# Split weight tiles start 64 or 192 bytes behind a 256-byte edge where they are stationary

## The chip, the cores and the metric

The kernel runs on one core of one Trainium2 chip. The metric is the device time of one execution in microseconds; three runs of the kernel before gave 2508.59, 2505.05 and 2508.44 us, so the median is 2508.44 us.

## The reference, cut to what matters

The reference is two transformer blocks in float32 on 256 tokens of width 2048. The first block is a sliding-window attention and a gated feed-forward layer of width 5632. The second block has an mLSTM layer and then a banded attention. Nearly all of the work is products of the 256 x 2048 activations with large weight matrices. Those whose product the change touches are the query and key columns of `w_in` in the mLSTM layer, the key columns of `kv_w`, and both halves of the attention's `w_in`:

```
def mlstm_mixer(h, w_in, conv_w, conv_b, gate_b, g_head, w_out):
    proj = h @ w_in
    qk = silu(causal_conv(proj[..., :A_V0], conv_w, conv_b))     # query and key columns
    v, o, z = proj[..., A_V0:A_O0], proj[..., A_O0:A_Z0], proj[..., A_Z0:A_G0]
    ...
    return y @ w_out

def second_block(x, c, ...):
    ...
        kv = hkv @ kv_w
        k_sh, v_sh = kv[..., :B_WIDTH], kv[..., B_WIDTH:]
        y = band_attention_mixer(h, k_sh, v_sh, b_w_in[j], b_rel[j], b_w_out[j])
    x = x + gate * rmsnorm(y, g_post[l])

def band_attention_mixer(h, k, v, w_in, rel_table, w_out):
    qz = h @ w_in
    q, z = qz[..., :B_WIDTH], qz[..., B_WIDTH:]
    o = chunk_band_attention(q, k, v, rel_table)
    return (o * silu(z)) @ w_out
```

## The kernel before, in words

**The products.** A weight matrix is read in chunks of 512 columns (`CW`), and a chunk in slots of 256 rows, each one DMA of 512 KB on SyncE's queue into a tile `w` (128 partitions, two row blocks of 512 columns, 4096 bytes in a partition; three buffers). `stream_split` makes two float32r tiles of each: ScalarE copies `w` to `wh`, VectorE writes the remainder `w - wh` to `wl` (four buffers each). The activations lie split in the same way, as `xh` and `xl` for what comes from the residual and `ah` and `al` for what comes from within a layer; each of these holds 16 blocks of 128 x 256 values, 1024 bytes in a partition per block. TensorE then makes three products per pair of blocks: high by high, high by low and low by high.

**The two modes.** `products` (L267) has two orders. In mode "tok" a block of activations (128 tokens) is stationary, that is loaded into TensorE, and 512 weight columns are streamed past it. In mode "wst" it is the other way round: 128 columns of `wh` or `wl` are stationary and the 256 tokens of `xh` or `xl` are streamed, so that the result comes out transposed. Every matmul has a load of its own. Twenty chunks are of mode "wst", each of 16 row blocks x 4 column groups x 3 products = 192 matmuls: eight of query and key columns (`qk_done`, one for each mLSTM head), four of keys (`k_done`) and eight of queries and gates (`qb_done`, `zb_done`). All other chunks are "tok".

**The names in the profile.** A row names the tile written, then the streamed tile, then the loaded one: `mm<-xh,wh` is "wst" (`xh` streams, `wh` is loaded), `mm<-wh,xh` is "tok". `bg` is the PSUM tile of everything else: transposes, attention, and the column sums of `mv_reduce` (L390), in which `acch` and `accl` stream past the constant `onesr`. Since every engine call passes through the wrapper `Eng`, nearly all rows have the line L66.

**Order and addresses.** The order of all instructions is worked out while the program is built: `do_group` takes the slots one after another, and a small model of the engines' clocks (`Clock`, `Eng`) decides between which matmuls the background tasks stand. It knows the shapes and not the addresses. In a partition the tiles of the pool `keep` come first, then those of `strm` (`w`, `wh`, `wl`, `mvt`), then `rest`, `small` and a pool per layer. In the built program all of `xh`, `xl`, `ah`, `al`, `wh` and `wl` start on a multiple of 256 bytes, and so does each block or column group of them that a matmul of a chunk reads. `onesr` starts 128 bytes behind such an edge, `acch` and `accl` 192 bytes.

**The end.** After the last chunks `fin_half` (L1235) squares each PSUM result on ScalarE to get its sum of squares (`sumsq`, L458); the squares themselves go to a scratch tile `sq` of the layer's pool that nobody reads.

Of the kernel before, what the change touches and what calls it, by code (L numbers as in the profile page):

```python
# [10 lines left out]
F32 = mybir.dt.float32  # L11
F32R = mybir.dt.float32r
# [6 lines left out]
P = 128  # L19
# [2 lines left out]
KD = D // P  # L22
SL = 2
CW = 512
NEG = -1.0e30
EPS = 1e-6
DFF = 5632
# [53 lines left out]
def kernel(ctx: ExitStack, tc: tile.TileContext, i: dict, out: bass.AP):  # L81
# [6 lines left out]
    strm = ctx.enter_context(tc.tile_pool(name="strm", bufs=1))  # L88
    rest = ctx.enter_context(tc.tile_pool(name="rest", bufs=1))
    small = ctx.enter_context(tc.tile_pool(name="small", bufs=4))  # L90
    psp = ctx.enter_context(tc.tile_pool(name="psp", bufs=8, space=PSUM))

    live = [0, 0]
    mmres = [4]
    ver = {"x": [0] * KD, "a": [0] * KD}
# [21 lines left out]
    xh = keep.tile([P, KD, T], F32R, name="xh")  # L117
# [15 lines left out]
    order = []  # L133
# [4 lines left out]
    def stream_load(upto):  # L138
        while cnt["load"] < min(upto, len(order)):
            ch, s = order[cnt["load"]]  # L140
            w = strm.tile([P, SL, CW], F32, tag="w", bufs=3, name="w")
            ch.load(s, w)
# [3 lines left out]
    def stream_split(upto):  # L146
        while cnt["split"] < min(upto, len(order)):
            j = cnt["split"]
            w = loaded.pop(j)
            clk.cur = 0.0  # L150
            wh = strm.tile([P, SL, CW], F32R, tag="wh", bufs=4, name="wh")
            S.copy(wh, w)
            wl = strm.tile([P, SL, CW], F32R, tag="wl", bufs=4, name="wl")
            V.tensor_sub(wl, w, wh.bitcast(F32))
            split[j] = (wh, wl, clk.cur)
            cnt["split"] += 1
# [54 lines left out]
    def wload(w, r0, c0):  # L211
        def f(s, t):
            a = w[r0 + s * SL * P:r0 + (s + 1) * SL * P, c0:c0 + CW]
            nc.sync.dma_start(out=t, in_=a.rearrange("(k p) n -> p k n", p=P))
# [11 lines left out]
    def do_group(idxs):  # L226
        staged = len(idxs) > 1
        ch, s0 = order[idxs[0]]
        for k in range(s0 * SL, (s0 + len(idxs)) * SL):
            while ver[ch.need[0]][k] < ch.need[1][k]:  # L230
                stall()
        stream_load(idxs[0] + 1 + PF)
        stream_split(idxs[0] + 1 + SP)
        if s0 == 0:
            shp = [P, CW] if ch.mode == "tok" else [P, 2, T]
            while live[0] + live[1] > 6:
# [3 lines left out]
        for ts in ((0,), (1,)) if staged else ((0, 1),):  # L240
            for j, idx in enumerate(idxs):
                s = order[idx][1]
                if j and ts[0]:
                    stream_load(idx + 1 + PF)
                    stream_split(idx + SP)
                wh, wl, t_w = split.pop(idx) if ts[-1] else split[idx]
                for k in range(SL):
                    kt = s * SL + k
                    clk.cur = max(t_w, rdy[ch.need[0]][kt])
                    products(ch, kt, k, wh, wl, ts)  # L250
                    ch.k = kt + ts[-1]
                    if not staged:
                        mv_step()
                    if kt < ch.nk - 1:
                        pump()
            if s == ch.ns - 1:
                clk.cur = clk.eng["pe"]
                if ch.part is not None:
                    for t in ts:
                        ch.part(ch.ps, t)  # L260
                if ts[-1]:
                    if not (ch.done and ch.done(ch.ps)):
                        mm_free()
                    ch.ps = None
                pump()
# [52 lines left out]
    def mv_jobs():  # L318
        for lab, w, c0, b, kind, dst in (
                [("A", i["ada0"], j * CW, i["ada_b"][0:1, j * CW:(j + 1) * CW], "col", (0, j // 4, j % 4))  # L320
                 for j in range(8)]
# [134 lines left out]
        return b.rearrange("p a b -> p (a b)")  # L456

    def sumsq(junk_pool, src, dst, scale=1.0):  # L458
        j = junk_pool.tile([P, CW], F32, tag="sq", bufs=1, name="sq")
        S.activation(j, src, ACTF.Square, scale=scale, accum_out=dst)  # L460

    def xt_pair(m):
# [83 lines left out]
    ssx = rest.tile([P, 2, 4], F32, name="ssx")  # L546
# [208 lines left out]
    def resid(n, ps, pool, after):  # L755
        for t in range(2):
            c = x[:, t, n * CW:(n + 1) * CW]
            V.tensor_add(c, ps[t], c)
            sumsq(pool, c, ssx[:, t, n:n + 1])
        add_bg(after(n))  # L760
# [36 lines left out]
    pools = {}  # L797
# [50 lines left out]
    def down_part(ps, t):  # L848
        c = x[:, t, 3 * CW:]
        V.tensor_add(c, ps[t], c)  # L850
        sumsq(pools["q2"], c, ssx[:, t, 3:4])
        if t:
            add_bg(xt_raw(3, raw))
# [146 lines left out]
    def num_task(h, v):  # L1000
# [22 lines left out]
        for t in range(2):  # L1023
            sumsq(q3, nm[t], ss[:, t:t + 1], scale=rd[:, t:t + 1])
# [143 lines left out]
    def band_head(g, j):  # L1168
# [5 lines left out]
        nc.sync.dma_start(out=bi, in_=bass.AP(tensor=rel.tensor, offset=h * 383, ap=[[1, P], [1, T]]))  # L1174
        G.memset(bi[0:64, 0:64], NEG)
        yield 1
# [57 lines left out]

    def fin_half(ps, t, n):  # L1235
        c = pools["yy"][:, t, n * CW:(n + 1) * CW]
        sumsq(pools["q4"], ps[t], ssx[:, t, n:n + 1])
        V.tensor_mul(c, ps[t], gt[1][:, n * CW:(n + 1) * CW])

    def fin_done(n):  # L1240
        def f(ps):
            for t in range(2):
                fin_half(ps, t, n)
        return f

    def fin_part(ps, t):
        fin_half(ps, t, 3)
        x_rstd((t,))
        for n in range(4):
            c = x[:, t, n * CW:(n + 1) * CW]  # L1250
            y = pools["yy"][:, t, n * CW:(n + 1) * CW]
            if n == 3:
                S.activation(y, y, ACTF.Copy, scale=rst[:, t:t + 1])
                G.tensor_add(c, c, y)
            else:
                V.scalar_tensor_tensor(c, y, rst[:, t:t + 1], c, op0=ALU.mult, op1=ALU.add)
        for n in range(4):
            nc.sync.dma_start(out=out[t * P:(t + 1) * P, n * CW:(n + 1) * CW], in_=x[:, t, n * CW:(n + 1) * CW])
# [39 lines left out]
    S.activation(warm, ones[:, 0:1], ACTF.Exp)  # L1298
    stream_load(1)
    stream_split(1)  # L1300
    load_x(0)
    nc.sync.dma_start(out=cols, in_=i["cols"])
# [35 lines left out]
def _lay(inputs):  # L1338
# [10 lines left out]
    r = np.arange(P)  # L1349
    lo = np.where(r[None, :] <= r[:, None], f(0), f(NEG)).astype(f)  # L1350
    up = np.where(r[None, :] > r[:, None], f(0), f(NEG)).astype(f)
    ge = np.where(r[None, :] >= r[:, None], f(0), f(NEG)).astype(f)
    inv = np.power(10000.0, -np.arange(0, 64, 2) / 64.0).astype(f)
# [33 lines left out]
```

## Time and profile before

| | |
|---|---|
| median of three runs | 2508.44 us |
| the profiled execution, its own time | 2509.79 us |
| its span, first to last instruction | 2508.0 us |
| mean granted clock of TensorE | 0.989 |
| TensorE busy: matmuls, loads | 2438.4 us (97%), 2076.4 us (83%) |
| VectorE, ScalarE, GpSimd busy | 1752.8 us (70%), 1210.1 us (48%), 173.4 us (7%) |
| share of the matmuls in the chain that ended last | 77% |

"PE" is TensorE's matmuls, "PEld" its loads, which overlap them. A matmul's row lasts from its start until its result is out, and the next one starts long before that; the pace of a run of matmuls is therefore read from their starts and not from their durations. [...]

### The profile page before, as it was taken

Reading aid. Unit: us, or ns where it says so; the run is one execution under the profiler, and the core shown is the slowest. Engines: PE = TensorE matmul, PEld = TensorE weight load, DVE = VectorE, ACT = ScalarE, POOL = GpSimd, SP = SyncE. Lnnn points to the kernel's source line nnn. Section 1 sums busy time; section 2 is a strip of 40 time slices with the busy share of each in tenths; the row PEclk is TensorE's granted clock in tenths of the full one; section 3 lists DMA queues with packets and bytes.
Section 4 is the critical chain, followed back from the end, with each engine's and each line's share of the span. In section 5 each row is a group of like instructions: output and inputs, shape, how many; then the busy total and the mean of one; then the engine's idle time right before and its main releaser. Section 6 shows DMA issues by size and latency. Waiting matters only on the chain.

```text
span 2508.0 us, 34570 instructions
## 1 busy us (share of the span) xinstructions
PE 2438.4 (97%) x12782; PEld 2076.4 (83%) x12782; DVE 1752.8 (70%) x2577; ACT 1210.1 (48%) x1654; POOL 173.4 (7%) x174
## 2 busy tenths in 40 slices
PE   8989999999999999899999999999999899999998
PEld 6867888887888888778888788888888789899986
DVE  6885777777777777768778777755454664577765
ACT  5665544334443444554445444445444544555553
POOL 0232000000000000201101100101101120000000
PEclk9989999999999999999999999999999999999999
DMA  6524788888888887568878788856556456678854
GB/s 211 157 96 143 238 285 284 286 275 279 287 283 291 285 286 267 159 213 269 264 250 273 267 286 277 261 170 192 182 169 196 151 151 186 193 254 263 259 188 153
DMA packets 319226, 575.63 MB, mean 230 GB/s; under 512 B 21680, under 2 KB 56752, under 8 KB 319056
## 3 DMA queue, kind: packets, MB, share of 16 engines
q1 hardware_dynamic: 319056, 573.42, 70.8%
q8 instruction: 100, 1.64, 0.3%
q14 instruction: 70, 0.57, 0.1%
HBM read 571.25 MB, written 2.10 MB: 229 GB/s over the span
## 4 chain that ended last, share of the span: by engine, by line
PE 77%; DVE 7%; DMA 6%; issue 4%; ACT 4%; POOL 2%; SPq 0%; ACTq 0%; DVEq 0%; POOLq 0%
PE mm L66 72%; PE bg L66 5%; DVE wl L66 3%; ACT wh L66 2%; DMA w<-in_a_w_in_dram 2%; DVE mvacc L66 2%; DMA w<-in_w_gate_dram 1%; DMA w<-in_w_down_dram 1%; POOL big L66 1%; DMA w<-in_w_qkv_dram 1%; ACT big L66 1%; POOL y L66 0%; DMA w<-in_a_w_out_dram 0%; POOL so L66 0%; ACT sq L66 0%
## 5 line engine op out<-in xcount | busy, mean ns | idle before, releaser
L66 DVE TENSOR_TENSOR wl<-w,wh 128x1024 fp32r<-128x1024 f32 x816 | 1009.3, 1244 | 620.9 <-ACT wh L66 605.4
L66 ACT CAST wh<-w 128x1024 fp32r<-128x1024 f32 x816 | 854.9, 1051 | 957.1 <-PE mm L66 598.8
L66 PE MATMUL mm<-wh,xh 128*128 128x512 f32 x1760 | 691.4, 393 | 0.0
L66 PE MATMUL mm<-wh,xl 128*128 128x512 f32 x1760 | 686.8, 390 | 3.8 <-DVE xl L66 3.8
L66 PE MATMUL mm<-wl,xh 128*128 128x512 f32 x1760 | 686.8, 390 | 3.0 <-DVE wl L66 3.0
L66 DVE SCALAR_TENSOR_TENSOR mvacc<-mvt,sc,mvacc 128x512 f32<-128x512 f32 x512 | 392.2, 766 | 10.1 <-issue 0.5
L66 PEld LDWEIGHTS mm<-wh,xl 128*128 128x128 f32 x1760 | 331.1, 188 | 74.3 <-DVE xl L66 4.7
L66 PEld LDWEIGHTS mm<-wl,xh 128*128 128x128 f32 x1760 | 331.2, 188 | 72.2 <-DVE wl L66 5.1
L66 PEld LDWEIGHTS mm<-wh,xh 128*128 128x128 f32 x1760 | 331.2, 188 | 70.5 <-issue 2.6
L66 PE MATMUL mm<-xh,wh 128*128 128x256 f32 x1280 | 370.0, 289 | 7.9 <-DVE xh L66 7.9
L66 PE MATMUL mm<-xl,wh 128*128 128x256 f32 x1280 | 367.5, 287 | 1.0 <-DVE xl L66 0.9
L66 PE MATMUL mm<-xh,wl 128*128 128x256 f32 x1280 | 365.6, 286 | 0.0
L66 PE MATMUL mm<-wh,al 128*128 128x512 f32 x864 | 337.8, 391 | 3.5 <-DVE al L66 3.5
L66 PE MATMUL mm<-wh,ah 128*128 128x512 f32 x864 | 340.3, 394 | 0.0
L66 PE MATMUL mm<-wl,ah 128*128 128x512 f32 x864 | 337.5, 391 | 0.0
L66 PEld LDWEIGHTS mm<-xh,wh 128*128 128x128 f32 x1280 | 249.2, 195 | 11.6 <-DVE xh L66 5.5
L66 PEld LDWEIGHTS mm<-xl,wh 128*128 128x128 f32 x1280 | 249.1, 195 | 4.4 <-DVE xl L66 3.5
L66 PEld LDWEIGHTS mm<-xh,wl 128*128 128x128 f32 x1280 | 249.1, 195 | 0.0
L66 PEld LDWEIGHTS mm<-wh,al 128*128 128x128 f32 x864 | 163.0, 189 | 38.1 <-DVE al L66 3.9
L66 PEld LDWEIGHTS mm<-wh,ah 128*128 128x128 f32 x864 | 162.9, 189 | 36.7 <-issue 3.3
L66 PEld LDWEIGHTS mm<-wl,ah 128*128 128x128 f32 x864 | 163.0, 189 | 33.2 <-DVE wl L66 0.3
L66 POOL TENSOR_TENSOR so<-so,sz 128x512 f32<-128x512 f32 x16 | 29.6, 1851 | 711.8 <-DVE mvacc L66 361.8
(191 smaller groups left out, 1303.2 us busy)
## 6 DMA issues: line engine op xcount, KB each, us to landing
mvt<-in_ada_dram SPq DMA_DIRECT2D x192, 512.0 KB
w<-in_a_w_in_dram SPq DMA_DIRECT2D x192, 512.0 KB
w<-in_w_gate_dram SPq DMA_DIRECT2D x88, 512.0 KB
w<-in_w_up_dram SPq DMA_DIRECT2D x88, 512.0 KB
w<-in_w_down_dram SPq DMA_DIRECT2D x88, 512.0 KB
mvt<-in_kv_ada_dram SPq DMA_DIRECT2D x64, 512.0 KB
w<-in_a_w_in_dram SPq DMA_DIRECT2D x128, 256.0 KB
w<-in_a_w_out_dram SPq DMA_DIRECT2D x64, 512.0 KB
```

Of the source, the lines that this page charges most:

```text
L66: return fn(*a, **k)
```

## The change

The buffers of `wh` and `wl` become 256 bytes longer in each partition (`ROOM`, 64 values of four bytes). For a slot of a "wst" chunk the tile that is written and read begins 16 values (64 bytes) into its buffer if the slot's number is even, and 48 values (192 bytes) if it is odd; for a "tok" slot it begins at the buffer's start as before. The eight longer buffers take 2048 bytes more, so every tile behind them moves by 2048 bytes. To make room for that in the last layer, the squares of `fin_half` go into the first two blocks of `xh` instead of a scratch tile. In all five engines' orders the instructions, their shapes and their waits are the same before and after; eight squares name `xh` in place of `sq`. The `wh` and `wl` buffers lie 4352 bytes apart in place of 4096, all still on multiples of 256.

```
+ROOM = 64
+SHIFT = 16
...
+    def offset_tile(tag, off):
+        t = strm.tile([P, SL * CW + ROOM], F32R, tag=tag, bufs=4, name=tag)
+        return t[:, off:off + SL * CW].rearrange("p (k n) -> p k n", n=CW)
...
             j = cnt["split"]
             w = loaded.pop(j)
+            off = SHIFT * (1 + 2 * (j % 2)) if order[j][0].mode == "wst" else 0
             clk.cur = 0.0
-            wh = strm.tile([P, SL, CW], F32R, tag="wh", bufs=4, name="wh")
+            wh = offset_tile("wh", off)
             S.copy(wh, w)
-            wl = strm.tile([P, SL, CW], F32R, tag="wl", bufs=4, name="wl")
+            wl = offset_tile("wl", off)
             V.tensor_sub(wl, w, wh.bitcast(F32))
...
     def sumsq(junk_pool, src, dst, scale=1.0):
-        j = junk_pool.tile([P, CW], F32, tag="sq", bufs=1, name="sq")
+        if junk_pool is None:
+            j = xh[:, 0:2].rearrange("p k t -> p (k t)")
+        else:
+            j = junk_pool.tile([P, CW], F32, tag="sq", bufs=1, name="sq")
         S.activation(j, src, ACTF.Square, scale=scale, accum_out=dst)
...
     def fin_half(ps, t, n):
         c = pools["yy"][:, t, n * CW:(n + 1) * CW]
-        sumsq(pools["q4"], ps[t], ssx[:, t, n:n + 1])
+        sumsq(None, ps[t], ssx[:, t, n:n + 1])
```

## Rows read from the trace of the kernel before

**Rows 1.** The page: span, busy times, GB/s by slice, the chain that ended last.
```profile
span 2508.0 us, 34570 instructions
PE 2438.4 (97%) x12782; PEld 2076.4 (83%) x12782; DVE 1752.8 (70%) x2577; ACT 1210.1 (48%) x1654; POOL 173.4 (7%) x174
...
GB/s 211 157 96 143 238 285 284 286 275 279 287 283 291 285 286 267 159 213 269 264 250 273 267 286 277 261 170 192 182 169 196 151 151 186 193 254 263 259 188 153
...
PE 77%; DVE 7%; DMA 6%; issue 4%; ACT 4%; POOL 2%; SPq 0%; ACTq 0%; DVEq 0%; POOLq 0%
```

**Rows 2.** TensorE's waits, by what ended them: us in total, times, longest.
```profile
PE bg L66 <- POOL y L66: 8.6, 5, 2.2
PE mm L66 <- DVE xh L66: 7.9, 13, 1.9
```

**Rows 3.** Stretches: length, busy us (instructions) by engine, clock, DMA share, GB/s.
```profile
1136.80:1145.40 8.60, 8.60 (x74) 8.60 (x72) 7.04 (x5) 6.45 (x7) 5.04 (x3) 1.00 0.85 278
...
1521.00:1546.00 25.00, 25.00 (x205) 24.71 (x204) 18.49 (x23) 11.44 (x15) 0.53 (x1) 1.00 0.90 289
2040.00:2110.00 70.00, 70.00 (x582) 69.82 (x581) 29.41 (x24) 29.10 (x32) 0.00 (x0) 1.00 0.63 189
2220.00:2408.00 188.00, 187.25 (x1547) 185.62 (x1546) 142.33 (x272) 102.74 (x171) 3.58 (x18) 1.00 0.77 250
```

**Rows 4.** Loads with `xh`, "wst", 2040 to 2105: ns min/median/max, first and last start.
```profile
L66 PEld LDWEIGHTS mm<-xh,wl x181: 192/192/192, 2040.0 to 2104.8; 128*128 128x128 f32 x181
L66 PEld LDWEIGHTS mm<-xh,wh x181: 192/192/192, 2040.2 to 2105.0; 128*128 128x128 f32 x181
```

**Rows 5.** The same in a "tok" stretch, 2110 to 2190.
```profile
L66 PEld LDWEIGHTS mm<-wh,xh x118: 187/188/188, 2110.2 to 2189.8; 128*128 128x128 f32 x118
```

**Rows 6.** The loads of `onesr` for `acch` and for `accl`, whole span, same columns.
```profile
L66 PEld LDWEIGHTS bg<-acch,onesr x16: 186/192/192, 1487.0 to 2400.9; 128*128 128x128 f32 x16
L66 PEld LDWEIGHTS bg<-accl,onesr x16: 186/188/286, 1487.2 to 2401.0; 128*128 128x128 f32 x16
```

**Rows 7.** Loads grouped, 1534.99 to 1536.2: xcount, busy us, mean ns, idle before.
```profile
L66 PEld LDWEIGHTS mm<-xh,wh 128*128 128x128 f32 x4 | 0.8, 188 | 0.0
L66 PEld LDWEIGHTS mm<-xl,wh 128*128 128x128 f32 x3 | 0.6, 188 | 0.0
L66 PEld LDWEIGHTS mm<-xh,wl 128*128 128x128 f32 x3 | 0.6, 187 | 0.0
```

**Rows 8.** Matmuls in time in that stretch: start us, us.
```profile
1534.95 0.28 PE L66 MATMUL bg<-acch,onesr 128*128 128x256 f32 x1
...
1536.38 0.28 PE L66 MATMUL mm<-xl,wh 128*128 128x256 f32 x1
```

**Rows 9.** Loads grouped, 1536.5 to 1545.
```profile
L66 PEld LDWEIGHTS mm<-xh,wl 128*128 128x128 f32 x24 | 4.6, 192 | 0.0
```

**Rows 10.** Matmuls in time, a "tok" stretch behind transposes.
```profile
256.54 0.39 PE L66 MATMUL mm<-wl,ah 128*128 128x512 f32 x1
...
258.85 0.39 PE L66 MATMUL mm<-wh,al 128*128 128x512 f32 x1
```

**Rows 11.** Loads grouped, 2220 to 2408, the chunks of queries and gates.
```profile
L66 PEld LDWEIGHTS mm<-xl,wh 128*128 128x128 f32 x445 | 85.2, 191 | 0.2
```

**Rows 12.** Splits by tile, ns min/median/max: at an edge, then 192 bytes behind one.
```profile
L66 ACT CAST ah<-yb x16: 397/406/407, 2250.3 to 2423.9; 128x256 fp32r<-128x256 f32 x16
L66 DVE TENSOR_TENSOR al<-yb,ah x16: 424/426/427, 2250.8 to 2424.4; 128x256 fp32r<-128x256 f32 x16
...
L66 ACT CAST acch<-mvacc x16: 400/406/408, 1484.4 to 2398.2; 128x256 fp32r<-128x256 f32 x16
L66 DVE TENSOR_TENSOR accl<-mvacc,acch x16: 409/416/427, 1485.6 to 2398.7; 128x256 fp32r<-128x256 f32 x16
```

**Rows 13.** ScalarE's squares of the last chunks, and its casts of `wh`, same columns.
```profile
L66 ACT ACTIVATE sq<-mm x8: 597/598/599, 2447.8 to 2497.8; 128x512 f32<-128x512 f32 x8
...
L66 ACT CAST wh<-w x816: 1027/1053/1078, 4.7 to 2486.6; 128x1024 fp32r<-128x1024 f32 x164
```

**Rows 14.** The transposes of `y` in one query-and-key chunk: start us, us, wait before.
```profile
1145.40 0.27 PE L66 MATMUL bg<-kc,y 128*128 128x128 f32 x1
1147.79 0.98 PE L66 MATMUL bg<-kc,y 128*128 128x128 f32 x7 [2.12 <-POOL y L66]
```

## The prediction

> **What bounds the kernel now.** I read the page first, then the waits, then stretches of time by mode. The reader is to see that TensorE is hardly ever without work: its matmuls are busy for 97% of the span and make up 77% of the chain that ended last [rows 1], and its longest sums of waits are 8.6 and 7.9 us [rows 2]. In the four "wst" chunks of keys it works without a pause at clock 1.00, with 582 matmuls in 70 us [rows 3]. So the time is mostly the number of matmuls times the pace at which they start, and the change can act on the pace only.
>
> The pace of a "wst" stretch comes from the first and last starts: between the loads at 2040.2 and 2105.0 us lie 180 intervals of three matmuls, and 64.8 us / 540 is 120.0 ns [rows 4]. In "tok" 79.6 us / 351 is 226.8 ns [rows 5]. [...] The loads differ: in "wst" each one lasts 192 ns, minimum as maximum, in "tok" 187 to 188 [rows 4, 5]. In "wst" the streaming needs less than the pace, and the next matmul follows its load at a steady distance, 192 - 120 = 72 ns. There I take the load to be what sets the pace: a load of 188 ns would give 116.
>
> **The change part by part.** The term that matters is where the loaded columns lie relative to the streamed ones. Before, both start at an edge in every chunk; after, the loaded ones start 64 or 192 bytes behind it in "wst". The trace never shows that pair, but it shows three near it, where `mv_reduce` streams `acch` and `accl` (192 bytes behind an edge) past `onesr` (128):
> - `onesr` is loaded while `xh` or `wh` streams, distance 128: median 192 ns, as at distance 0 [rows 6].
> - `onesr` is loaded once more while `acch` streams, distance 64: median 188 ns [rows 6].
> - `wh` is loaded while `accl` streams, distance 192: it is the first of four with mean 188 [rows 7].
>
> So distances 0 and 128 go with 192 ns and distances 64 and 192 with 188. The change puts every "wst" load at one of the latter two. A weakness of this reading is that the loads behind such a pair stay at 187 to 188 ns although they are back at distance 0, ten of them [rows 7], and only then return to exactly 192 [rows 9]. What I see may thus be a rhythm that was disturbed and not a distance that is good. The bounds of the new pace: 116 ns by the load (188 - 72), and 119 by the starts of the disturbed stretch (12 intervals in 1.43 us [rows 8]). I take 117, nearer to the load, since the starts include the return to the old rhythm; that is 3 ns less for a matmul.
>
> How many matmuls gain: of the 20 "wst" chunks the first of query and key columns and the first of keys run while VectorE still writes `xh`, with 13 waits on it [rows 2], and what they gain there is waited away. The other 18 have 18 x 192 = 3456 matmuls, and 3456 x 3.0 ns = 10.4 us. Two things are subtracted:
> - In five heads TensorE waits for GpSimd's `y` in the middle of the query-and-key chunk (8.6 us in all [rows 2]; one such place in [rows 14]). In that chunk 74 matmuls stand before the first transpose [rows 3]. Reaching the wait sooner gives nothing: 5 x 74 x 3 ns = 1.1 us.
> - In the eight chunks of queries and gates the mean load is already 85.2 / 445 = 191.5 ns [rows 11], half a nanosecond below 192: 8 x 192 x 0.5 = 0.8 us.
>
> That leaves 8.5 us. Feeding the faster matmuls: in the query-and-key chunks the DMA engines move 289 GB/s at 0.90 busy [rows 3]; at 117 ns they would have to move 296. If 293, the highest of the page's slices [rows 1], were a ceiling, seven chunks would stop at 118.4 ns and 7 x 192 x 1.4 ns = 1.9 us would be lost. I take nothing, since three buffers stand ahead and the "tok" chunks behind need less, and keep 1.9 us for the range.
>
> The smaller parts. The splits write to 64 or 192 behind an edge: a cast of 256 columns takes 406 ns at an edge and 406 at 192 behind it, the subtraction 426 and 416 [rows 12]; zero, and ScalarE and VectorE have slack anyway (103 and 142 us busy in 188 [rows 3]). The eight squares write float32r in place of float32: 598 ns for 512 columns from PSUM now, and a cast that writes float32r takes 1053 for 1024 [rows 13], so the new type costs between nothing and -0.1 us each, of which only the last two lie on the path at the end; zero. They wait for nothing new, as `xh` was last streamed by 2408 us and the first square starts at 2447.8 [rows 13]. The shift of all later tiles by 2048 bytes leaves every distance modulo 256 as it was. The streamed `wh` of "tok" now starts at odd multiples of 256 in two buffers of four; a distance of 128 made no difference to a load, so I take zero for 256.
>
> **The sum.** 2509.79 (the profiled execution, 1.35 above the median) - 8.5 = 2501.3, and against the median 2508.44 - 8.5 = 2499.9; I forecast 2500.
>
> [...]
>
> **The rivals.**
> - The rhythm stays. If 120 ns belongs to the start of a matmul and not to the distance, the "wst" stretches settle at 120 again whatever the offset, and the time is 2508. [...] Against it: distance 64 and 192 show 188 in the very load that has it. That the offset does not do what it says is this case too.
> - Slower. The new offset puts the loads into a worse rhythm and keeps them there. The trace knows such a one: behind transposes a "tok" stretch starts its matmuls at 10 intervals in 2.31 us, 231 ns, 4 above its steady 226.8 [rows 10]. Kept through "wst" that is 3456 x 4 = +13.8 us, 2522. It decides from 1.5 ns per matmul (5 us / 3456). Against it: no disturbed "wst" load in [rows 7] is above 192.
> - A still lower rhythm. The shortest loads are 186 ns [rows 6], so 114: 6 ns x 11 chunks x 192 = 12.7 us outside the query-and-key chunks, and 2.2 us in those if 118.4 is their floor; less the 1.9 us subtracted above, some 13 us, 2495.
>
> **How the numbers follow.** I give the forecast 55%, the rhythm that stays 29%, the slower one 10%, the still lower one 6%. About 0.2%, 5 us, is what a measurement of this kernel can tell from no change. The forecast's own range goes from 116 ns (-12 us, 2496) to 119 with the DMA ceiling (-2.5, 2505.5); roughly one in fifteen of it falls short of 5 us. So faster 0.57, same 0.33, slower 0.10. The range of 8 in 10 runs from 2492, which takes in the lower rhythm and some scatter, to 2511, which takes in the whole of no change with the spread of three runs (3.5 us) and the beginning of the slower case.
>
> **What would show it.** In the profile after, the loads of the key chunks have a median of 187 to 188 ns in place of 192, the 582 matmuls of such a stretch take some 68 us and not 70, and the "tok" stretches keep 226.8 ns. The gain lies in the 18 chunks, 0.5 to 0.6 us each. Loads of 192 at the new offset would prove the first rival, loads above 192 the slower one. The prediction is wrong too if "wst" gains and the waits on `y`, on VectorE or on the weights' DMAs grow by as much, or if "tok" changes its pace.

## The result and the profile after

The changed kernel took 2492.54 us (median of four runs, 2489.58 to 2496.67), the kernel before on the same chip 2506.78 us (four runs, 2505.05 to 2508.59). The ratio is 0.9949 with a 95% interval of 0.9931 to 0.9966, that is a gain of 8.5 to 17.3 us, 12.8 in the middle; the medians differ by 14.2. The forecast was faster, 2500 us, in a range of 2492 to 2511. Sign and range held, the range only just (the median lies 0.5 us above its lower end), and the gain is larger than the 8.5 us forecast. The profiled execution after took 2491.55 us, 18.2 us less than the profiled one before (which lay 3 us above the median it is compared with here).

The page of the kernel after: span, busy times, and the engines' shares of the chain that ended last. Two lines more stand at the top of this kernel, so its rows have L68 where those before have L66.

```profile
span 2489.8 us, 34570 instructions
PE 2418.9 (97%) x12782; PEld 2057.6 (83%) x12782; DVE 1754.3 (70%) x2577; ACT 1209.0 (49%) x1654; POOL 173.6 (7%) x174
...
PE 81%; DVE 6%; DMA 4%; issue 4%; ACT 3%; POOL 2%; SPq 0%; DVEq 0%; ACTq 0%; POOLq 0%
```

Against [rows 1] the instructions are the same in number, TensorE is busy for 19.5 us less, VectorE, ScalarE and GpSimd for the same time as before. TensorE's matmuls still have by far the largest share of the chain, and their busy time got shorter by about what the span got shorter. The next fence has three stretches of the kernel after, with the columns of [rows 3]: a query-and-key chunk, the last three chunks of keys (the first one has waits), and the chunks of queries and gates.

```profile
1516.00:1541.00 25.00, 25.00 (x209) 24.55 (x208) 19.13 (x26) 12.63 (x17) 0.53 (x1) 1.00 0.90 288
2031.00:2095.00 64.00, 64.00 (x568) 64.00 (x567) 29.28 (x24) 27.25 (x29) 0.00 (x0) 1.00 0.66 201
2210.00:2390.00 180.00, 177.90 (x1513) 175.57 (x1512) 140.75 (x272) 100.89 (x171) 3.56 (x18) 1.00 0.79 255
```

In the key chunks 568 matmuls now start in 64 us, where 582 took 70: at the new pace 582 would take 65.6 us, 4.4 less. The clock is 1.00 in each stretch, as it was. Now the loads in the key chunks, in the form of [rows 4], with those of the "tok" stretch behind, in the form of [rows 5].

```profile
L68 PEld LDWEIGHTS mm<-xh,wl x174: 187/188/188, 2031.0 to 2089.8; 128*128 128x128 f32 x174
L68 PEld LDWEIGHTS mm<-xh,wh x174: 187/188/188, 2031.1 to 2089.9; 128*128 128x128 f32 x174
...
L68 PEld LDWEIGHTS mm<-wh,xh x111: 187/188/188, 2100.0 to 2174.8; 128*128 128x128 f32 x111
```

In "wst" 58.8 us / (173 x 3) is 113.3 ns, 6.7 below the 120.0 of before, with loads of 188 ns in place of 192. In "tok" 74.8 us / (110 x 3) is 226.7 ns: unchanged. But 113.3 is not the pace of every "wst" chunk. Two short stretches of an early query-and-key chunk, loads and then matmuls, run otherwise:

```profile
L68 PEld LDWEIGHTS mm<-xh,wl x6: 187/188/188, 1133.0 to 1134.8; 128*128 128x128 f32 x6
...
L68 PE MATMUL mm<-xh,wh x12: 280/281/281, 1131.8 to 1135.7; 128*128 128x256 f32 x12
```

3.9 us / (11 x 3) is 118 ns, with the same loads of 188 ns. What differs is the row of the matmul itself, 281 ns here. In the key chunks of the kernel after, and in those of the kernel before, it has these lengths:

```profile
L68 PE MATMUL mm<-xh,wh x174: 276/276/277, 2030.8 to 2089.7; 128*128 128x256 f32 x174
```

```profile
L66 PE MATMUL mm<-xh,wh x181: 283/283/283, 2039.9 to 2104.7; 128*128 128x256 f32 x181
```

So there are two steady rhythms at the new offsets, 113.3 ns (rows of 276) and 117.8 ns (rows of 281 here), and one at the old offset, 120.0 ns (283). Over all intervals of 110 to 126 ns that begin with a "wst" matmul the mean went from 119.82 ns (3683 of them) to 115.10 (3689): 4.72 ns x 3689 = 17.4 us. "tok" has 227.08 before and 227.07 after.

TensorE's waits of the kernel after, as in [rows 2]: the one on GpSimd's `y` grew by 2.1 us, the one on `xh` by 0.9 (0.8 of it in the first key chunk).

```profile
PE bg L68 <- POOL y L68: 10.7, 5, 2.8
PE mm L68 <- DVE xh L68: 8.8, 10, 2.2
```

The 18.2 us between the two profiles are not all of the change. The first "wst" matmul started at 1023.4 us before and at 1019.1 after, so 4.3 us were ahead of everything that the offset touches. Most of them are a wait on `sg` in the profile before, 3.2 us at 592 us, which does not appear after:

```profile
PE bg L66 <- DVE sg L66: 3.2, 2, 2.9
```

From the first "wst" matmul on, the kernel after was 13.9 us shorter: 17.4 us of pace, less the 3.0 us by which the two waits grew, are 14.4, and the medians differ by 14.2.

### The profile page after: what moved, and what is told of

Its sections match the earlier page's. It is cut to its first block, busy times and chain, and to the rows that moved or that the text cites. A ratio compares the mean times of both kernels' runs of the same rounds, so it can differ in the third digit from the quotient of the medians.

```text
span 2489.8 us, 34570 instructions
## 1 busy us (share of the span) xinstructions
PE 2418.9 (97%) x12782; PEld 2057.6 (83%) x12782; DVE 1754.3 (70%) x2577; ACT 1209.0 (49%) x1654; POOL 173.6 (7%) x174
## 4 chain that ended last, share of the span: by engine, by line
PE 81%; DVE 6%; DMA 4%; issue 4%; ACT 3%; POOL 2%; SPq 0%; DVEq 0%; ACTq 0%; POOLq 0%
PE mm L68 76%; PE bg L68 5%; DVE wl L68 2%; DMA w<-in_a_w_in_dram 2%; ACT wh L68 2%; DVE mvacc L68 1%; POOL big L68 1%; DMA w<-in_w_qkv_dram 1%; POOL so L68 0%; POOL y L68 0%; DMA w<-in_a_w_out_dram 0%; ACT sq L68 0%; ACT big L68 0%; DMA mvacc<-in_ada_b_dram 0%; DVE xl L68 0%
## 5 line engine op out<-in xcount | busy, mean ns | idle before, releaser
L68 DVE TENSOR_TENSOR wl<-w,wh 128x1024 fp32r<-128x1024 f32 x816 | 1010.0, 1245 | 603.6 <-ACT wh L68 590.0
L68 ACT CAST wh<-w 128x1024 fp32r<-128x1024 f32 x816 | 854.9, 1052 | 941.6 <-PE mm L68 633.3
L68 PE MATMUL mm<-wh,xl 128*128 128x512 f32 x1760 | 687.3, 390 | 4.7 <-DVE xl L68 4.7
L68 PE MATMUL mm<-wh,xh 128*128 128x512 f32 x1760 | 691.6, 393 | 0.0
L68 PE MATMUL mm<-wl,xh 128*128 128x512 f32 x1760 | 687.0, 390 | 2.5 <-DVE wl L68 2.5
L68 DVE SCALAR_TENSOR_TENSOR mvacc<-mvt,sc,mvacc 128x512 f32<-128x512 f32 x512 | 392.9, 767 | 10.1 <-DMA mvacc<-in_ada_b_dram 0.9
L68 PEld LDWEIGHTS mm<-wh,xl 128*128 128x128 f32 x1760 | 331.1, 188 | 75.2 <-DVE xl L68 5.9
L68 PEld LDWEIGHTS mm<-wl,xh 128*128 128x128 f32 x1760 | 331.3, 188 | 72.6 <-DVE wl L68 4.9
L68 PEld LDWEIGHTS mm<-wh,xh 128*128 128x128 f32 x1760 | 331.4, 188 | 70.3 <-issue 2.9
L68 PE MATMUL mm<-xh,wh 128*128 128x256 f32 x1280 | 363.6, 284 | 8.8 <-DVE xh L68 8.8
L68 PE MATMUL mm<-xl,wh 128*128 128x256 f32 x1280 | 360.7, 282 | 0.9 <-DVE xl L68 0.7
L68 PE MATMUL mm<-xh,wl 128*128 128x256 f32 x1280 | 359.2, 281 | 0.0
L68 PE MATMUL mm<-wh,al 128*128 128x512 f32 x864 | 337.6, 391 | 4.9 <-DVE al L68 4.9
L68 PE MATMUL mm<-wh,ah 128*128 128x512 f32 x864 | 339.8, 393 | 0.0
L68 PE MATMUL mm<-wl,ah 128*128 128x512 f32 x864 | 337.3, 390 | 0.0
L68 PEld LDWEIGHTS mm<-xh,wh 128*128 128x128 f32 x1280 | 244.8, 191 | 11.9 <-DVE xh L68 6.2
L68 PEld LDWEIGHTS mm<-xl,wh 128*128 128x128 f32 x1280 | 244.8, 191 | 3.8 <-DVE xl L68 3.3
L68 PEld LDWEIGHTS mm<-xh,wl 128*128 128x128 f32 x1280 | 244.5, 191 | 0.0
L68 PEld LDWEIGHTS mm<-wh,al 128*128 128x128 f32 x864 | 162.8, 188 | 39.6 <-DVE al L68 5.3
L68 PEld LDWEIGHTS mm<-wh,ah 128*128 128x128 f32 x864 | 162.8, 188 | 36.6 <-issue 3.3
L68 PEld LDWEIGHTS mm<-wl,ah 128*128 128x128 f32 x864 | 162.7, 188 | 33.2 <-DVE wl L68 0.3
L68 POOL TENSOR_TENSOR so<-so,sz 128x512 f32<-128x512 f32 x16 | 30.6, 1911 | 707.0 <-DVE mvacc L68 360.3
```

Of the source, the lines that this page charges most:

```text
L68: return fn(*a, **k)
```

## The experiments

**Theory and rivals at this point.** Theory: the pace is set by where the loaded columns lie relative to the streamed ones, modulo 128 (0 and 128 alike, 64 and 192 alike). Rivals: what counts is the absolute address of the loaded columns; or any distance but 0 helps; or the alternation from slot to slot is what helps; or the gain is one of the by-products (the longer buffers, the moved tiles, the squares in `xh`).

**Offsets by themselves.** A kernel of matmuls alone: runs of 144 with 256 streamed columns ("wst") and of 96 with 512 ("tok"), all operands in SBUF, each run disturbed beforehand by four or five float32 matmuls. Its core:

```
+    for off in OFFS:                      # 0, 16, 32, ..., 128, 192 bytes
+        for r in range(2):
+            disturb(4 + r)
+            wst(6, [off], 0)              # loaded at off, streamed at 0
+    for offs, mov in (([64, 192], 0), ([0, 128], 0), ([0], 64), ([64], 64)):
...
+    for off in OFFS:
+        for r in range(2):
+            disturb(4 + r)
+            tok(8, off)
```

> Nothing of the blocks is computed here: the kernel holds only runs of matmuls of the two modes, with the loaded columns at an offset of 0, 16, 32, 48, 64, 80, 96, 112, 128 and 192 bytes behind a 256-byte edge, each run behind a few fp32 matmuls; also the streamed columns at 64 with the loaded ones at 0 and at 64, and offsets in turn (64/192 and 0/128). Distance theory (only the distance of the loaded from the streamed columns counts, modulo 128): 120 ns at 0 and 128, 113 to 118 at 64 and 192, the same 113 to 118 with the streamed ones at 64 and the loaded ones at 0, and 120 again with both at 64. Disturbance theory (a change of offset keeps the rhythm from settling): 120 at every constant offset after some ten matmuls, below 118 only with offsets in turn, and there for 0/128 too. For runs of 512 streamed columns both say 226.7 at 0 and 128; the distance theory leaves open whether 64 gives 220 or stays at 226.7.

The pace in the second half of each run (ns, two runs each), from the starts:

| loaded columns at (streamed at 0) | 256 streamed | 512 streamed |
|---|---|---|
| 0 | 120.0, 120.0 | 226.7, 226.7 |
| 16 | 118.3, 118.4 | 233.3, 226.7 |
| 32 | 118.4, 118.4 | 233.3, 233.3 |
| 48 | 123.2, 117.8 | 233.4, 233.3 |
| 64 | 113.3, 117.8 | 233.3, 233.3 |
| 80; 96; 112, twice the same within 0.1 | 118.8; 117.3; 120.0 | 232.0; 234.3; 233.3 |
| 128 | 118.6, 118.6 | 232.4, 232.2 |
| 192 | 117.8, 117.8 | 228.8, 228.8 |
| 64 and 192 in turn, by slot | 113.3, 113.3 | |
| 0 and 128 in turn, by slot | 118.9, 118.9 | |
| 0, streamed at 64 | 117.8, 113.3 | |
| 64, streamed at 64 | 120.0, 120.0 | |

Matmuls of this kernel, one tile of each run; `w064h` is loaded at offset 64, `m064h` streamed at 64. In this order: 0; 64, first and second run; 128; streamed at 64; both at 64.

```profile
L86 PE MATMUL mm<-m000h,w000h x42: 283/283/283, 49.9 to 64.7; 128*128 128x256 f32 x42
...
L86 PE MATMUL mm<-m000h,w064h x45: 276/276/276, 194.9 to 209.9; 128*128 128x256 f32 x45
...
L86 PE MATMUL mm<-m000h,w064h x44: 281/281/281, 212.8 to 228.0; 128*128 128x256 f32 x44
...
L86 PE MATMUL mm<-m000h,w128h x43: 279/281/285, 338.9 to 353.8; 128*128 128x256 f32 x43
...
L86 PE MATMUL mm<-m064h,w000h x44: 276/276/276, 500.1 to 514.7; 128*128 128x256 f32 x44
...
L86 PE MATMUL mm<-m064h,w064h x42: 283/283/283, 518.0 to 532.8; 128*128 128x256 f32 x42
```

The kernel's three rhythms are all here, with VectorE, ScalarE and GpSimd at 0.00 us and the DMA engines at 0.01 of their time at most in these stretches, and with the same lengths of rows: 283, 276, 281. Both at 64 is as both at 0 (120.0 ns), and either of the two may be moved (113.3 and 117.8): the distance counts and not the address. Modulo 128 was wrong: at distance 128 the intervals walk between 115 and 122 ns with a mean of 118.6. Distance 64 twice gave two different paces, each steady to the end of its run. The two runs differ in the number of float32 matmuls ahead, so I read the pace as a matter of how a run was entered. And with 512 columns no offset is better than none: 64 gave 233.3 ns, neither of the two values (220 and 226.7) that the theory had left open.

**One offset for all slots, and none.** Three kernels that differ from the kernel after in one line:

```
-            off = SHIFT * (1 + 2 * (j % 2)) if order[j][0].mode == "wst" else 0
+            off = SHIFT if order[j][0].mode == "wst" else 0          # 64
+            off = 2 * SHIFT if order[j][0].mode == "wst" else 0      # 128
+            off = 0 if order[j][0].mode == "wst" else 0              # 0
```

> The changed kernel with the offset 64 for every wst slot instead of 64 and 192 in turn. Distance theory: about as the changed kernel, 2487 to 2497, wst at 113 to 118 ns. Disturbance theory: wst settles at 120, about 2507.

> The changed kernel with the offset 128 for every wst slot. Distance theory: distance 128 is as 0, wst stays at 120.0 ns and the time at 2505 to 2509. If any offset from the edge of the buffer did it: 2487 to 2497.

> The changed kernel with no offset: the longer buffers, the shift of all later tiles by 2048 bytes and the squares written to xh alone. Distance theory: 120.0 ns and 2505 to 2509. If the gain came from these by-products: 2487 to 2497.

One run each, with the kernel before at 2505.78 us on the same chip: 2492.88 at 64, 2504.08 at 128, 2505.28 at 0. The mean "wst" intervals were 116.15, 119.02 and 119.82 ns. With 0 the time and the pace are those of before, so the longer buffers, the moved tiles and the squares cost and bring nothing that shows. Since its buffers lie 4352 bytes apart, loads at even and at odd multiples of 256 take turns in it, and its key chunks still run at 120 ns: it is the distance modulo 256 that counts. The key chunks at 64, matmuls and loads:

```profile
L68 PE MATMUL mm<-xh,wh x188: 281/281/281, 2028.7 to 2094.8; 128*128 128x256 f32 x188
...
L68 PEld LDWEIGHTS mm<-xh,wl x188: 187/188/188, 2028.8 to 2094.9; 128*128 128x128 f32 x188
```

66.1 us / (187 x 3) = 117.8 ns: entered in the slower rhythm, these chunks kept it to their end, where the kernel after has 113.3. Other chunks of the same kernel ran at 113.3. The key chunks at 128:

```profile
L68 PE MATMUL mm<-xh,wh x189: 279/281/285, 2036.9 to 2103.9; 128*128 128x256 f32 x189
...
L68 PEld LDWEIGHTS mm<-xh,wl x189: 187/188/189, 2037.0 to 2104.0; 128*128 128x128 f32 x189
```

Here the loads last 188 ns too, and the pace is 67.0 / (188 x 3) = 118.8 with matmuls that walk between 279 and 285. So a load of 188 ns does not give the gain, and 128 is neither as 0 nor as 64.

**Does alternation tip the rhythm?** A second kernel of matmuls alone, with four disturbances for each pattern (one to four float32 matmuls ahead). A pattern gives the offsets of the high and of the low part for slot `s` of 24 matmuls and its half `k`:

```
+        lambda s, k: (64, 64),
+        lambda s, k: (192, 192),
+        lambda s, k: (64, 64) if s % 2 == 0 else (192, 192),
...
+        lambda s, k: (64, 192),
+        lambda s, k: (64, 192) if s % 2 == 0 else (192, 64),
+        lambda s, k: (64, 64) if k == 0 else (192, 192),
...
+    for pat in pats:
+        for r in range(4):
+            disturb(1 + r)
+            wst(6, pat)
```

> Again only runs of matmuls, nothing of the blocks. Runs of 256 streamed columns, each pattern behind four different disturbances: loaded columns at 64, at 192, at 64 and 192 in turn by slot of 24 matmuls (beginning with either), high parts at 64 and low parts at 192 (the same in every slot, or exchanged by slot), 64 and 192 in turn by half slot, and at 56, 60, 68 and 72. Two-rhythms theory (at distance 64 or 192 there are two steady rhythms, 113.3 and 117.8 ns, the entry chooses, and a change of offset at a slot's edge tips the slower into the faster): constant 64 and 192 show 113.3 in some runs and 117.8 in others and keep it, offsets in turn end in 113.3 in all of their runs. Distance-alone theory (the change of offset does nothing): in turn shows the same mixture as constant. Offsets of 56 to 72 lie between the 123.3 or 117.8 of 48 and the 118.8 of 80 unless they share the rhythm of 64. Runs of 512 columns with low parts elsewhere than high parts, or all at 224 or 240: at or above 226.7; a value of 220 would be a new rhythm.

Constant 64 ended at 117.8, 117.8, 113.3 and 113.3 ns behind one, two, three and four float32 matmuls (four had given 113.3 in the first kernel too, and five 117.8), constant 192 at 117.8 all four times, as it did twice in the first kernel; there the expectation of both rhythms failed. In turn by slot, either way round, all eight runs ended at 113.3 and had a mean of 114.0 to 116.2 over the whole run. With high and low parts at different offsets all eight ended at 113.3, within some 12 matmuls, with means of 114.0 to 114.3; in turn by half slot all four did, with means of 114.0 to 114.7. Offsets of 56, 60, 68 and 72 gave 117.8, 119.4, 118.3 and 118.3, and no mixture helped with 512 columns (226.7 to 233.3). The moment of tipping can be seen in the first kernel, in slots at 64, 192, 64 and 192:

```profile
L86 PE MATMUL mm<-m000h,w064h x5: 281/281/281, 411.0 to 412.4; 128*128 128x256 f32 x5
...
L86 PE MATMUL mm<-m000h,w192h x5: 280/280/280, 413.8 to 415.2; 128*128 128x256 f32 x5
...
L86 PE MATMUL mm<-m000h,w064h x2: 276/276/277, 415.6 to 415.9; 128*128 128x256 f32 x2
...
L86 PE MATMUL mm<-m000h,w192h x6: 276/276/276, 419.0 to 420.7; 128*128 128x256 f32 x6
```

At the first edge, from 64 to 192, the slower rhythm stays (281, then 280). At the second, from 192 to 64, the rows go to 276, and they stay there when the next slot is at 192 again. It is so in all runs with slots or half slots in turn: of ten changes from 192 to 64 in the 117.8 rhythm eight ended in 113.3, of six changes from 64 to 192 none did, and no change ended the 113.3 rhythm. In the trace of the kernel after, counted where neither another matmul nor a wait stands near the edge, 24 of 32 changes from 192 to 64 ended in 113.3 and none of 16 from 64 to 192; of 54 changes met in 113.3 none left it. Where one slot ran at 113.3 and the next at 117.8, a matmul of `bg` (a transpose, a column sum, attention) or a wait stood in between each time. So the change of offset pulls a chunk back into the faster rhythm after such a break has thrown it out.

**The offset in "tok" too.**

```
-            off = SHIFT * (1 + 2 * (j % 2)) if order[j][0].mode == "wst" else 0
+            off = SHIFT * (1 + 2 * (j % 2))
```

> The changed kernel with the offsets 64 and 192 in turn for the tok slots too, where the weights are streamed and the activations loaded (distance 192 or 64). Distance theory with the paces measured in bench_offsets (233.3 at 64 and 228.9 at 192 against 226.7 at 0): 4.4 ns more for each of 7872 tok matmuls, 35 us, less what waits swallow: 2515 to 2530. If the loads behind an edge were good in both modes: below 2490. If the offset acts only where the weights are loaded: 2487 to 2497.

One run of it took 2517.99 us, with the kernel before at 2503.83: 14.2 slower than before, where the kernel after was 14.2 faster by the medians on its chip, so some 28 us lie between them. A "tok" stretch of it and the last "wst" matmuls ahead of that:

```profile
L68 PE MATMUL mm<-wh,xh x105: 388/391/398, 2117.6 to 2189.6; 128*128 128x512 f32 x105
...
L68 PE MATMUL mm<-xh,wl x53: 276/276/277, 2099.8 to 2117.5; 128*128 128x256 f32 x53
```

72.0 us / (104 x 3) = 230.8 ns in "tok", while "wst" keeps its 113.3. Over the whole kernel "tok" has a mean of 230.93 against 227.08; 3.85 ns x 7740 such intervals = 29.8 us, about what was lost. The same distance that helps when 256 columns stream costs when 512 do.

**High and low parts at different offsets, timed.** If a change of offset tips the rhythm, changes within the slot should tip it soonest:

```
-            off = SHIFT * (1 + 2 * (j % 2)) if order[j][0].mode == "wst" else 0
+            off = SHIFT if order[j][0].mode == "wst" else 0
...
-            wl = offset_tile("wl", off)
+            wl = offset_tile("wl", 3 * off)
```

It ran in five rounds on one chip with the kernel after once more and the one with 64 throughout.

> The changed kernel with the high parts of every wst slot at 64 and the low parts at 192, in place of both at 64 or both at 192 by slot. Two-rhythms theory: an offset that changes within the slot tips the rhythm into 113.3 ns within some ten matmuls instead of at a slot's edge, as in bench_patterns (means of 114.0 to 114.3 with the entry): wst at about 114 where the changed kernel has 115.1, 3690 x 1.1 ns = 4 us, so 2486 to 2490 against 2490 to 2494. If the changed kernel is held by waits elsewhere by now: the same as the changed kernel.

> The changed kernel once more, beside the others on one chip: about 14 us below the kernel before, wst at 115 ns.

> The constant offset 64, timed. Two-rhythms theory: 116.15 ns a wst matmul in its first profile against 115.1 with offsets in turn: 1 ns x 3690 = 4 us slower than the changed kernel, some 10 us below the kernel before. If the offset in turn adds nothing: equal to the changed kernel within 1 us.

| kernel | median us | ratio to before, 95% interval | mean "wst" ns | span of its profile |
|---|---|---|---|---|
| high at 64, low at 192 | 2492.83 | 0.9938 (0.9926 to 0.9949) | 113.80 | 2487.4 |
| the kernel after (in turn by slot) | 2495.72 | 0.9962 (0.9948 to 0.9977) | 115.11 | 2490.7 |
| 64 throughout | 2497.47 | 0.9955 (0.9943 to 0.9967) | 115.71 | 2495.7 |

The paces and their order are the expected ones. The times are not: the first two medians lie 3 and 2 us above the ranges expected (2486 to 2490, 2490 to 2494), and the kernel after is 11.9 us below the kernel before here, not 14. One of its six runs took 2505.89 us at a mean granted clock of 0.938, where the other five had 0.985 to 0.989; it is part of its interval, and the median of the other five is 2495.08. Matmuls in a chunk of queries and gates, first with high and low parts apart, then the kernel after in the same place:

```profile
L68 PE MATMUL mm<-xh,wh x57: 276/276/276, 2181.7 to 2200.8; 128*128 128x256 f32 x57
```

```profile
L68 PE MATMUL mm<-xh,wl x59: 276/276/283, 2182.7 to 2202.7; 128*128 128x256 f32 x59
```

In the first no row leaves 276 ns; in the second the slower rhythm shows as a maximum of 283. By the pace the first is worth 1.3 ns x 3689 = 4.8 us, by the medians 2.9 us. The intervals of these two just touch, so the time alone hardly tells them apart; pace, profile and median agree that it is the fastest of the three. Between 64 throughout and in turn by slot the times tell nothing, only the pace does (0.6 ns, 2.2 us).

## Why the prediction was right, and where it was not

- **What bounds.** Right: the pace of the matmuls is the time. From the first "wst" matmul on the profile got 13.9 us shorter, and pace less the grown waits is 14.4.
- **That the distance matters in "wst".** Right, and shown: moving either operand gives the gain (113.3 or 117.8 ns), moving both takes it away (120.0), the by-products alone do nothing (119.82 before and with offset 0). The distance does not set one pace, though: with the loaded columns at 64 and the streamed ones at 0 both 113.3 and 117.8 occurred, with both at 0 only 120.0. The rival of a rhythm that stays at 120 fell. For this form of matmul the offset alone gave 113.3 to 123.2 ns; what in TensorE makes the difference, no run shows.
- **The term of 3.0 ns a matmul.** This is the step that was mis-sized: 117 ns forecast, 115.1 measured. In the 18 chunks that were counted the mean went from 119.85 to 115.02 ns, so the 10.4 us were 16.7. The mean is a mixture of 113.3, below the bound of 116 and near the rival of a still lower rhythm (114), and 117.8, inside the bounds. I had weighed forecast and rival against each other; both happened, in different stretches of one run.
- **"I take the load to be what sets the pace."** Wrong. It gave the bound of 116 by 192 - 72. That the streaming needs less than the 120.0 ns of before is shown: matmuls of 256 columns started 113.3 ns apart in the kernel after. But loads of 188 ns go with 113.3, with 117.8 and, at distance 128, with 118.8 ns, so the 72 is not a fixed distance: load less pace is 74.7, 70.2 and 69.2 there. The 188 ns are a sign that the steady rhythm of 120 was left and no measure of the new one. The matmul's own row comes nearer: 276 ns at 113.3, 279 to 281 at 117.8, 283 at 120.0. The 0.8 us subtracted for queries and gates came from the load as well; their pace before was 119.75 ns, only 0.25 below 120.
- **"Distances 0 and 128 go with 192 ns."** Wrong as a statement on steady runs: 128 gives 118.6 to 119.0 ns and loads of 188. The 192 of `onesr` [rows 6] was one load that followed on a stretch at 120, and showed that stretch's rhythm. The weakness named in the text, that a disturbed rhythm and a good distance look alike in single loads, was a real one: distance 64 and 192 were read rightly from rows that could not bear it alone, and that much of the forecast was luck.
- **What was subtracted.** The waits on `y` took back 2.1 us (1.1 forecast at 3 ns; 5 x 74 x 4.7 ns would be 1.7), the waits on `xh` 0.9. The two chunks left out of the count gained 0.09 and 0.04 us from first to last start, as forecast. The DMA ceiling was misread: the highest slice in [rows 1] is 291 GB/s and not 293, which would make it 119.2 ns and 2.9 us. It did not bite: the seven chunks ran at a mean of 115.7 ns, below either floor, and in 25 us 209 matmuls stand beside 288 GB/s and 0.90 busy, where 205 had 289.
- **The smaller parts.** Right: the squares take 597 ns (598 before), "tok" keeps its 227.1 ns, and offset 0 with everything else of the change gives the time of before.
- **What would show it.** Loads of 187 to 188 in the key chunks and 226.7 in "tok" came; 582 matmuls would take 65.6 us, not 68 (the stretch holds three key chunks, not four); by their paces the 18 chunks gained from 0.6 to 1.3 us each in place of 0.5 to 0.6.
- **The slower rival.** It did not come in "wst". It is what the same offset does in "tok": 3.85 ns more on each matmul, close to the 4 that the disturbed stretch of [rows 10] had shown behind transposes.

## What to carry to other kernels

Where a row of matmuls runs back to back and each has its own load, measure the pace from first and last start of a long stretch, and try the distance between loaded and streamed columns modulo 256 bytes: here 64 and 192 together are worth 4 to 5% of the pace at 256 streamed columns (from 119.82 to 115.10 or 113.80 ns) and cost 2% at 512 (from 227.08 to 230.93), so each order of the operands needs its own offset. A single load or matmul behind a disturbance showed the rhythm it came from as much as its own addresses: ten loads back at distance 0 took 187 to 188 ns behind the column sums [rows 7], where steady ones take 192 [rows 4]; a long run of one kind settles it. If the good rhythm depends on how a stretch is entered, change the offset within the stretch; here high parts at 64 and low parts at 192 did it (113.80 ns, against 115.11 in turn by slot).

## What was not expected of the hardware

- At one and the same distance there are two steady rhythms, 113.3 and 117.8 ns; each lasted through a whole run of 144 matmuls, and 117.8 through some 560 in the key chunks at 64. A change from 192 to 64 tipped the second into the first in eight of ten cases, a change from 64 to 192 in none of six, and neither was seen to do the reverse. At a constant 192 only 117.8 was seen (six runs); the 113.3 was kept there when a slot at 64 had brought it, and it came once in two runs with the streamed columns at 64 and the loaded ones at 0.
- The steady paces lie on a grid of 6.67 ns, the difference between 120.0 and 113.3 and between 233.3 and 226.7: 113.3, 120.0, 226.7 and 233.3 ns are 17, 18, 34 and 35 such steps, and 117.8 is 53 in three matmuls. With all operands at 0, 256 columns more take 16 steps more (18 and 34). Three of the offsets at which the intervals vary repeat them, and a whole repeat again lasts a whole number of steps: 48 with 256 columns (first run) alternates between 116 to 117 and 130 ns, 37 steps in two matmuls; 128 with 256 columns repeats after five, 89 steps; 192 with 512 columns after three, 103 steps. Why there are such steps, and why at distance 64 one fewer was measured at 256 columns (113.3 ns) and one more at 512 (233.3), no run here shows; it stays open.
- Within the offsets tried, a few bytes matter: 64 gave 113.3 or 117.8 ns, 60 gave 119.4 to 119.6, 48 gave 123.2 in one run and 117.8 in the other.
